# An attention head's 64-column copies ahead of the scores, its key turned in the scores' run, and two more tiles parked in DRAM

## The chip, the cores and the metric

The kernel runs on one core of a Trainium2 chip. Its time is the device time of one execution in microseconds. TensorE (PE, with its weight loads as PEld) does the matmuls, VectorE (DVE) and ScalarE (ACT) the elementwise work, GpSimd (POOL) and SyncE (SP) mostly issue DMA transfers. Each engine runs its own instruction stream in program order and waits for the others by semaphores.

## The reference

One layer of a decoder trunk, T = 1024 positions, D = 1024 channels, float32:

```
h = rms_norm(x, norm_w) * (1 + scale) + shift        # shift, scale, gate from c
hq, hf, hi, hz, gq, gk, gv, gz, ga, mg = split(h @ w_in)
HGRN, 8 heads, key 128, value 128:  f = lb + (1 - lb) * sigmoid(hf);  k = (1 - lb) * sigmoid(-hf);  q = silu(hq);  v = hi
GLA,  4 heads, key 128, value 256:  alpha = sigmoid(ga @ alpha_w + alpha_b) ** (1/16);  q = gq / sqrt(128);  k = gk;  v = gv
both: S_t = diag(decay_t) S_(t-1) + k_t v_t^T,   o_t = S_t^T q_t          # decay is f or alpha
y = rms_norm(o) * silu(z);   u = y @ w_branch
merged = sigmoid(mg_h) * u_h + sigmoid(mg_g) * u_g
out = rms_norm(x + gate * (merged @ w_out), final_norm_w)
```

The reference walks the recurrence in chunks of 64 positions. The kernel works with chunks of 128 (NCH = 8 of them) and splits them further, as told below.

## The kernel before

**Big matmuls.** A float32 product is taken as three fp32r products of high and low parts. The high part is a cast on ACT (L211), the low part a subtraction on DVE (L212). The input projection runs as a list of jobs (`Stream.jobs`); each job loads its weights with SP, splits them, and does runs of matmuls of 128 x 512 (L607, L2000), six of them to a unit. The branch products (L1422) and the output product (L1599) follow. All feature-major tiles of 128 x 1024 float32 live in 46 slots of SBUF (`Slots`, `S.get` and `S.free`); loads and splits of the next jobs (`Stream.ahead`) are only started while enough slots are free.

**Side work.** Between the units, `Stream.weave` advances generators. A generator gives back by `yield n` for how many units (divided by a pace of 1.08, for HGRN heads 1.15) it wants to be left alone. The twelve attention heads, four of GLA and then eight of HGRN, are such generators and run one after the other. A tile scheduler then sets the final order of the instructions on each engine; dependences become semaphore waits.

**One head** (`attention`, L639). q, k and the decays f stand feature-major, 128 x 1024. The scores within a chunk are built in levels, each with decays multiplied into q and k:

- L657 to L661: copies of q and products with decays go to the buffer `xb`; L665 is a run of matmuls for blocks of 4 positions.
- L667 to L694: q and k grow by decays, evictions into `blk`, the next products in `xb`; L698 is the run for blocks of 16.
- `keep(n)` copies the halves of k and q that face each other at level n with two ACT copies of 512 columns (L718) into `xb`. `grow(n)` then multiplies decays into k (L726), into q (L727), and shortens the totals (L729). In order: keep(16), grow(16), keep(32), grow(32).
- After waiting, and after `early` has asked for the values: three short runs of matmuls, for 16s (L756) and 32s (L762) on the copies, and for 64s (L767) on k and q themselves. Then grow(64), which has to wait for L767. Evictions: L771 on DVE, L776 (four) and L779 (two) on ACT, into `scT`.
- After `yield 3`: seven transposes of k (L791, TensorE against the identity) into two PSUM tiles, copied to `kT` by ACT (L792), and L795 (ACT). After `yield 2.5`: the state updates, L815 (kT times v) with L819 and L821 on DVE, and the outputs L834 and L836. For GLA, `inverse_root` follows (L992, L993 on TensorE, L994 and L995 on ACT, each behind a load of a table of functions).

**Other side work that shares the engines.** `alpha_side` makes the decays of the third and fourth GLA head: two DVE operations (L949, L950) per head, then on ACT exp (L953), ln (L956), exp (L960), both heads at each step. `gate_side` adds up the gate row with DVE operations (L1101, L1104), splits it (L202 on ACT, L203 on DVE) and sums it with four matmuls (L1112, L1113). `weight_sums` (L1266 to L1272, DVE) makes sums of weights for later. `gla_k_done` gets the key of a GLA head out of PSUM; of the fourth head (h = 3) it is written to DRAM and read back by `load_qk`, the third's stays in its slot. Decays of both stay in their slots (`alphas`).

Of the kernel before, what the change touches and what calls it, by code (L numbers as in the profile page):

```python
# [10 lines left out]
F32 = mybir.dt.float32  # L11
# [5 lines left out]
P = 128  # L17
D = 1024
T = 1024
KT = D // P  # L20
NCH = T // P
# [68 lines left out]
def hybrid_trunk_kernel(  # L90
# [6 lines left out]
    nc = tc.nc  # L97
# [541 lines left out]
    def attention(q, k, f, v, V, post, early, lead=3, next_up=None):  # L639
# [68 lines left out]
            return ap.rearrange("p (b two n) -> p b two n", two=2, n=n)  # L708

        flat = xb.rearrange("p b c -> p (b c)")  # L710
        kept = {}
        off = [320, tot[:, 256:320]]

        def keep(n):
            at = 0 if n == 16 else 1024
            kept[n] = flat[:, at:at + 512], flat[:, at + 512:at + 1024]
            for dst, src in zip(kept[n], (pairs(k, n)[:, :, 0, :], pairs(q, n)[:, :, 1, :])):
                nc.scalar.copy(dst.rearrange("p (b n) -> p b n", n=n), src)  # L718

        def grow(n):  # L720
            nb = T // (2 * n)
            at, cur = off
            cv = cur.rearrange("p (b two) -> p b two", two=2)
            left, right = cv[:, :, 0:1], cv[:, :, 1:2]
            qv, kv = pairs(q, n), pairs(k, n)
            TT(kv[:, :, 0, :], kv[:, :, 0, :], bc(right, [nb, n]), M)  # L726
            TT(qv[:, :, 1, :], qv[:, :, 1, :], bc(left, [nb, n]), M)  # L727
            nxt = tot[:, at:at + nb]
            TT(nxt.unsqueeze(2), left, right, M)  # L729
            off[:] = at + nb, nxt  # L730
# [13 lines left out]
        grow(16)  # L744
        keep(32)
        grow(32)
        yield 4
        early()
        yield 6 - lead
# [1 line left out]

        k16, q16 = kept[16]
        k32, q32 = kept[32]
        for b in range(32):
            ch, j = b // 4, b % 4
            nc.tensor.matmul(sc_ps[1][32 * j:32 * j + 16, ch * 16:ch * 16 + 16],  # L756
                             k16[:, b * 16:b * 16 + 16], q16[:, b * 16:b * 16 + 16], start=True, stop=True)
# [4 lines left out]
                nc.tensor.matmul(sc_ps[0][p0:p0 + 32, c0:c0 + 32], k32[:, i * 32:i * 32 + 32],  # L762
                                 q32[:, i * 32:i * 32 + 32], start=True, stop=True)
        for ch in range(NCH):
            s0 = ch * P
            p0, c0 = ch % 2 * 64, 128 + ch // 2 * 64
            nc.tensor.matmul(sc_ps[1][p0:p0 + 64, c0:c0 + 64], k[:, s0:s0 + 64],  # L767
                             q[:, s0 + 64:s0 + 128], start=True, stop=True)
        grow(64)
        cur = off[1]  # L770
        cpr(blk[:, :, 16:32], bc(masks[16], [NCH, 16]),  # L771
            sc_ps[1][:, 0:128].rearrange("p (c t) -> p c t", c=NCH))
        for hf in range(2):
# [5 lines left out]
            nc.scalar.copy(scT[0:64, odd::2, 64:128],  # L779
                           sc_ps[1][64 * odd:64 * odd + 64, 128:384].rearrange("p (c t) -> p c t", t=64))  # L780
        scoring.discard(me)
        yield 3


        kT = S.get([NCH, P])
        for g in range(2):
            nt = 4 if g == 0 else 3
            pt = mtile()
            for i in range(nt):
                ch = g * 4 + i  # L790
                nc.tensor.transpose(pt[:, i * P:(i + 1) * P], k[:, ch * P:(ch + 1) * P], ident)  # L791
            nc.scalar.copy(kT[:, g * 4:g * 4 + nt, :].rearrange("p c s -> p (c s)"), pt[:, 0:nt * P])  # L792
        S.free(k)
        for j in range(4):
            nc.scalar.copy(scT[32 * j:32 * j + 32, :, 32 * j:32 * j + 32], blk[32 * j:32 * j + 32])  # L795
        if next_up:
            next_up()
        yield 2.5
        per = 512 // V
        spp = 1024 // V  # L800
        st = [S.get([1024]) for _ in range((7 + spp - 1) // spp)]
# [107 lines left out]
    def alpha_half(half):  # L909
# [21 lines left out]
            nc.scalar.activation(alphas[h][:, sl], m[:, h, :], AF.Exp, scale=1.0 / TAU)  # L931
        S.free(z, m)

    def alpha_side(pair):
        zs = {}
        while len(S.free_list) < 6:
            yield 1
        for h in pair:
            zb = zs[h] = S.get([T])
            for th in range(2):  # L940
                pz = mtile()
                mm_alpha(pz, h, slice(th * 512, th * 512 + 512))
                nc.scalar.activation(zb[:, th * 512:(th + 1) * 512], pz, AF.Identity,
                                     bias=vec[:, R_AB + h:R_AB + h + 1])
            yield 2
        S.free(ga4, aw4)
        for h in pair:
            m = alphas[h] = S.get([T])
            nc.vector.tensor_scalar_min(m, zs[h], 0.0)  # L949
            nc.vector.scalar_tensor_tensor(zs[h], m, 2.0, zs[h], ALU.mult, ALU.subtract)  # L950
            yield 2
        for h in pair:
            nc.scalar.activation(zs[h], zs[h], AF.Exp)  # L953
        yield 3
        for h in pair:
            nc.scalar.activation(zs[h], zs[h], AF.Ln, bias=one_t)  # L956
            nc.vector.tensor_sub(alphas[h], alphas[h], zs[h])
            yield 2
        for h in pair:
            nc.scalar.activation(alphas[h], alphas[h], AF.Exp, scale=1.0 / TAU)  # L960
            S.free(zs[h])
        yield 3

    def silu_done(store, key):
# [80 lines left out]
                settle(qk, ("z", h, vh))  # L1045
        S.free(*sq.values())

    k3_d = dp.tile([P, T], F32, name="k3")

    def load_qk(h):  # L1050
        for f, key in ((h, "q"), (4 + h, "k")):
            if f < NG or h == 3:
                t = g_state[key, h] = S.get([T])
                nc.sync.dma_start(t, qk_d[f] if f < NG else k3_d)

    def gla_k_done(h):
        def f(ps):
            t = S.get([T])
            for th in range(2):
                nc.vector.tensor_copy(t[:, th * 512:th * 512 + 512], ps[th])  # L1060
            if h == 3:
                nc.gpsimd.dma_start(k3_d, t)
                S.free(t, sent=True)
            else:
                g_state[("k", h)] = t
        return f

    def col(c0, w=P):
# [1036 lines left out]
```

## Time and profile before

| | |
|---|---|
| runs | 1173.1, 1173.27, 1175.14 us (median 1173.27) |
| profiled execution | 1172.94 us, span 1171.2 us, granted clock 0.998 |
| busy | PE 98%, PEld 80%, DVE 72%, ACT 55%, POOL 12% of the span |
| seven transposes of a head (L791) | 84 in all, 11.1 us busy, 272 ns each |
| runs of L767 | 192 matmuls, 8.2 us busy, 228 ns each |
| ACT copies L718 | 0.62 us for 512 columns |
| DVE products L726, L727 | 0.69 us for 512 columns (mean) |

A row of the timeline has the start in us, the length, the engine, line and operation, the tile written and those read, and how many instructions the row joins; in brackets the time that the engine stood idle before it and what ended that. A row of the waits has who waited for what, the total in us, how often, and the longest.

### The profile page before, as it was taken

What the parts mean: (1) busy time and instruction counts of PE and PEld (TensorE: products, weight loads), DVE (VectorE), ACT (ScalarE), POOL (GpSimd) and SP (SyncE); (2) the same over time, 40 slices, a digit from 0 to 9 for tenths busy, and PEclk for the clock granted to TensorE, in tenths of its full rate; (3) what the DMA queues carried; (4) which work ended last, traced back from release to release, by engine and by line L of the source; (5) the groups of instructions that cost most, each with busy time, mean ns of one, the idle gap of its engine ahead of it and who ended that gap; (6) DMA issues with size and microseconds to landing.
All of it is one profiled execution on the core that took longest, in us unless ns stands there. A gap on an engine that the chain in (4) does not pass through costs nothing.

```text
span 1171.2 us, 20559 instructions
## 1 busy us (share of the span) xinstructions
PE 1147.1 (98%) x8089; PEld 942.8 (80%) x8089; DVE 841.5 (72%) x1316; ACT 646.4 (55%) x963; POOL 138.2 (12%) x285
## 2 busy tenths in 40 slices
PE   7999999999999999999999999999999999999997
PEld 5777888888778888788888888888888888888886
DVE  4755677676696636887697797595643866988994
ACT  5675464374574758646455446566643644534654
POOL 5121111010111101222211110001110000000000
PEclk9999999999999999999999999999999999999999
DMA  9847359486676546988766955146799746435523
GB/s 319 285 150 246 147 187 314 146 270 234 216 239 210 173 153 204 294 280 272 261 211 196 304 168 166 57 167 215 236 313 302 264 162 214 128 108 163 186 91 136
DMA packets 155986, 245.56 MB, mean 210 GB/s; under 512 B 10139, under 2 KB 107473, under 8 KB 155890
## 3 DMA queue, kind: packets, MB, share of 16 engines
q1 hardware_dynamic: 134866, 174.10, 47.3%
q0 software_dynamic: 20976, 70.15, 15.7%
q8 instruction: 63, 1.03, 0.4%
q14 instruction: 33, 0.27, 0.1%
q10 hardware_dynamic: 48, 0.01, 0.0%
HBM read 170.29 MB, written 73.92 MB: 209 GB/s over the span
## 4 chain that ended last, share of the span: by engine, by line
PE 81%; DVE 7%; ACT 7%; DMA 2%; issue 2%; SPq 1%; ACTq 0%; DVEq 0%
PE pd L607 18%; PE pd L2000 15%; PE pd L1422 14%; PE sc_ps L1422 6%; PE pm L1422 6%; PE pd L396 3%; PE pd L1599 3%; PE pm L834 2%; PE pm L836 2%; PE sc_ps L1599 2%; PE sc_ps L815 2%; PE sc_ps L396 1%; PE pm L1599 1%; ACT b L211 1%; DMA b<-in_ada_w_dram 1%
## 5 line engine op out<-in xcount | busy, mean ns | idle before, releaser
L607 PE MATMUL pd<-b,b 128*128 128x512 f32 x1248 | 299.7, 395 | 0.0
L607 PEld LDWEIGHTS pd<-b,b 128*128 128x128 f32 x1248 | 230.4, 188 | 48.8
L2000 PE MATMUL pd<-b,b 128*128 128x512 f32 x1008 | 238.5, 394 | 3.9 <-ACT b L211 2.4
L2000 PEld LDWEIGHTS pd<-b,b 128*128 128x128 f32 x1008 | 187.4, 188 | 46.0 <-ACT b L211 2.8
L1422 PE MATMUL pd<-b,b 128*128 128x512 f32 x720 | 169.4, 390 | 0.0
L1422 PEld LDWEIGHTS pd<-b,b 128*128 128x128 f32 x720 | 134.8, 188 | 28.2
L212 DVE TENSOR_TENSOR b<-b,b 128x1024 fp32r<-128x1024 f32 x92 | 110.7, 1220 | 55.0 <-ACT b L211 53.5
L1365 DVE TENSOR_TENSOR b<-b,b 128x1024 fp32r<-128x1024 f32 x56 | 68.1, 1220 | 55.1 <-ACT b L1364 43.7
L211 ACT CAST b<-b 128x1024 fp32r<-128x1024 f32 x92 | 93.6, 1047 | 18.0 <-DMA v<-b 4.1
L1364 ACT CAST b<-b 128x1024 fp32r<-128x1024 f32 x56 | 58.5, 1050 | 67.8 <-PE pm L1422 17.0
L1422 PE MATMUL sc_ps<-b,b 128*128 128x512 f32 x324 | 77.5, 390 | 0.1
L1342 DVE TENSOR_TENSOR b<-b,b 128x1024 fp32r<-128x1024 f32 x48 | 57.9, 1219 | 25.8 <-ACT b L1341 21.1
L1341 ACT CAST b<-b 128x1024 fp32r<-128x1024 f32 x48 | 49.9, 1049 | 42.8 <-PE pd L1422 15.8
L1422 PE MATMUL pm<-b,b 128*128 128x512 f32 x300 | 71.1, 389 | 0.0
L1422 PEld LDWEIGHTS sc_ps<-b,b 128*128 128x128 f32 x324 | 60.6, 188 | 12.9 <-ACT scT L779 0.5
L1422 PEld LDWEIGHTS pm<-b,b 128*128 128x128 f32 x300 | 56.3, 188 | 11.7
L203 DVE TENSOR_TENSOR b<-b,b 128x1024 fp32r<-128x1024 f32 (+1 forms) x37 | 35.7, 976 | 27.5 <-ACT b L202 27.3
L396 PE MATMUL pd<-b,b 128*128 128x512 f32 x192 | 51.8, 402 | 0.9 <-ACT b L202 0.8
L1274 POOL DMA_DIRECT2D ws<-b x64 | 34.6, 540 | 132.6 <-DVE b L1266 48.8
L726 DVE TENSOR_TENSOR b<-b,tot 128x512 f32<-128x512 f32 x36 | 24.7, 686 | 31.2 <-PE sc_ps L767 29.7
L834 PE MATMUL pm<-scT,b 128*128 128x128 f32 x256 | 46.8, 275 | 0.0
L396 PEld LDWEIGHTS pd<-b,b 128*128 128x128 f32 x192 | 34.3, 188 | 11.9 <-ACT b L202 1.8
(337 smaller groups left out, 1752.9 us busy)
## 6 DMA issues: line engine op xcount, KB each, us to landing
b<-in_w_in_dram SPq DMA_DIRECT2D x64, 512.0 KB, 6.1
ws<-b POOLq DMA_DIRECT2D x64, 256.0 KB, 5.1
b<-ws SPq DMA_DIRECT2D x32, 512.0 KB, 4.0
b<-in_w_in_dram SPq DMA_DIRECT2D x52, 256.0 KB, 4.5
b<-fx SPq DMA_DIRECT2D x24, 512.0 KB, 4.5
b<-in_x_dram SPq DMA_DIRECT2D x16, 512.0 KB, 6.1
b<-in_ada_w_dram SPq DMA_DIRECT2D x32, 256.0 KB, 6.4
v<-b POOLq DMA_DIRECT2D x32, 256.0 KB, 3.6
```

What stands on the lines that cost most here:

```text
L211: held(nc.scalar.copy(hi, src))
L212: nc.vector.tensor_sub(lo, src, hi.bitcast(F32))
L396: nc.tensor.matmul(accs[f], wg(a, d, f), b[d][:, half * 512:half * 512 + 512], start=(d == 0 and n == 0), stop=(d == KT - 1 and n == 2))
L607: nc.tensor.matmul(ps[th][0:w, :], a[:, k, 0:w], b[:, th * 512:(th + 1) * 512], start=(k == 0 and n == 0), stop=(k == KT - 1 and n == 2))
L834: nc.tensor.matmul(o, vch(ch)[:, vh * P:(vh + 1) * P], scT[:, ch, :], start=True, stop=(ch == 0))
L1341: nc.scalar.copy(hi, src)
L1342: nc.vector.tensor_sub(lo, src, hi.bitcast(F32))
L1364: nc.scalar.copy(hi, t)
L1365: nc.vector.tensor_sub(lo, t, hi.bitcast(F32))
L1422: nc.tensor.matmul(o, a[:, sl], c, start=(p in (1, 5) and kt == 0 and n == 0), stop=(kt == 3 and n == 2), skip_group_check=True)
L1599: nc.tensor.matmul(o, a, b, start=(p in (1, 5) and kt == 0 and n == 0), stop=(kt == 3 and n == 2), skip_group_check=True)
L2000: nc.tensor.matmul(st.bank[i], l_[:, i * P:(i + 1) * P], r_, start=(p in (1, 5) and kk == 0 and a == 0 and n == 0), stop=(kk == 1 and a == ...
```

## The change

It has three parts. `keep(64)` copies the 64-column halves into a buffer of its own (`wide`, one slot), and grow(64) follows at once, both directly behind grow(32); the matmuls of the 64s read the copies. The seven transposes come directly behind the matmuls of the 64s, in the same run on TensorE, so they read k after grow(64); their copies to kT come behind the score copies, and the two waits of 3 and 2.5 become one of 4. The third GLA head's key goes through DRAM as the fourth's did, and the fourth head's decay goes there too; `load_qk` reads them back.

```diff
--- before.py
+++ after.py
@@ -708,12 +708,16 @@
             return ap.rearrange("p (b two n) -> p b two n", two=2, n=n)
 
         flat = xb.rearrange("p b c -> p (b c)")
-        kept = {}
+        kept, wide = {}, []
         off = [320, tot[:, 256:320]]
 
         def keep(n):
-            at = 0 if n == 16 else 1024
-            kept[n] = flat[:, at:at + 512], flat[:, at + 512:at + 1024]
+            if n == 64:
+                wide.append(S.get([2, 512]))
+                kept[n] = wide[0][:, 0], wide[0][:, 1]
+            else:
+                at = 0 if n == 16 else 1024
+                kept[n] = flat[:, at:at + 512], flat[:, at + 512:at + 1024]
             for dst, src in zip(kept[n], (pairs(k, n)[:, :, 0, :], pairs(q, n)[:, :, 1, :])):
                 nc.scalar.copy(dst.rearrange("p (b n) -> p b n", n=n), src)
 
@@ -744,6 +748,9 @@
         grow(16)
         keep(32)
         grow(32)
+        keep(64)
+        grow(64)
+        cur = off[1]
         yield 4
         early()
         yield 6 - lead
@@ -751,6 +758,7 @@
 
         k16, q16 = kept[16]
         k32, q32 = kept[32]
+        k64, q64 = kept[64]
         for b in range(32):
             ch, j = b // 4, b % 4
             nc.tensor.matmul(sc_ps[1][32 * j:32 * j + 16, ch * 16:ch * 16 + 16],
@@ -762,12 +770,19 @@
                 nc.tensor.matmul(sc_ps[0][p0:p0 + 32, c0:c0 + 32], k32[:, i * 32:i * 32 + 32],
                                  q32[:, i * 32:i * 32 + 32], start=True, stop=True)
         for ch in range(NCH):
-            s0 = ch * P
             p0, c0 = ch % 2 * 64, 128 + ch // 2 * 64
-            nc.tensor.matmul(sc_ps[1][p0:p0 + 64, c0:c0 + 64], k[:, s0:s0 + 64],
-                             q[:, s0 + 64:s0 + 128], start=True, stop=True)
-        grow(64)
-        cur = off[1]
+            nc.tensor.matmul(sc_ps[1][p0:p0 + 64, c0:c0 + 64], k64[:, ch * 64:ch * 64 + 64],
+                             q64[:, ch * 64:ch * 64 + 64], start=True, stop=True)
+        S.free(*wide)
+        kT = S.get([NCH, P])
+        turned_k = []
+        for g in range(2):
+            pt = mtile()
+            for i in range(4 - g):
+                ch = g * 4 + i
+                nc.tensor.transpose(pt[:, i * P:(i + 1) * P], k[:, ch * P:(ch + 1) * P], ident)
+            turned_k.append(pt[:, 0:(4 - g) * P])
+        S.free(k)
         cpr(blk[:, :, 16:32], bc(masks[16], [NCH, 16]),
             sc_ps[1][:, 0:128].rearrange("p (c t) -> p c t", c=NCH))
         for hf in range(2):
@@ -779,23 +794,13 @@
             nc.scalar.copy(scT[0:64, odd::2, 64:128],
                            sc_ps[1][64 * odd:64 * odd + 64, 128:384].rearrange("p (c t) -> p c t", t=64))
         scoring.discard(me)
-        yield 3
-
-
-        kT = S.get([NCH, P])
-        for g in range(2):
-            nt = 4 if g == 0 else 3
-            pt = mtile()
-            for i in range(nt):
-                ch = g * 4 + i
-                nc.tensor.transpose(pt[:, i * P:(i + 1) * P], k[:, ch * P:(ch + 1) * P], ident)
-            nc.scalar.copy(kT[:, g * 4:g * 4 + nt, :].rearrange("p c s -> p (c s)"), pt[:, 0:nt * P])
-        S.free(k)
+        for g, pt in enumerate(turned_k):
+            nc.scalar.copy(kT[:, g * 4:g * 4 + 4 - g, :].rearrange("p c s -> p (c s)"), pt)
         for j in range(4):
             nc.scalar.copy(scT[32 * j:32 * j + 32, :, 32 * j:32 * j + 32], blk[32 * j:32 * j + 32])
         if next_up:
             next_up()
-        yield 2.5
+        yield 4
         per = 512 // V
         spp = 1024 // V
         st = [S.get([1024]) for _ in range((7 + spp - 1) // spp)]
@@ -931,6 +936,8 @@
             nc.scalar.activation(alphas[h][:, sl], m[:, h, :], AF.Exp, scale=1.0 / TAU)
         S.free(z, m)
 
+    alpha3_d = dp.tile([P, T], F32, name="alpha3")
+
     def alpha_side(pair):
         zs = {}
         while len(S.free_list) < 6:
@@ -959,6 +966,9 @@
         for h in pair:
             nc.scalar.activation(alphas[h], alphas[h], AF.Exp, scale=1.0 / TAU)
             S.free(zs[h])
+        if 3 in pair:
+            nc.gpsimd.dma_start(alpha3_d, alphas[3])
+            S.free(alphas.pop(3), sent=True)
         yield 3
 
     def silu_done(store, key):
@@ -1045,24 +1055,23 @@
                 settle(qk, ("z", h, vh))
         S.free(*sq.values())
 
-    k3_d = dp.tile([P, T], F32, name="k3")
+    k_d = {h: dp.tile([P, T], F32, name=f"k{h}") for h in (2, 3)}
 
     def load_qk(h):
         for f, key in ((h, "q"), (4 + h, "k")):
-            if f < NG or h == 3:
-                t = g_state[key, h] = S.get([T])
-                nc.sync.dma_start(t, qk_d[f] if f < NG else k3_d)
+            t = g_state[key, h] = S.get([T])
+            nc.sync.dma_start(t, qk_d[f] if f < NG else k_d[h])
+        if h == 3:
+            alphas[h] = S.get([T])
+            nc.sync.dma_start(alphas[h], alpha3_d)
 
     def gla_k_done(h):
         def f(ps):
             t = S.get([T])
             for th in range(2):
                 nc.vector.tensor_copy(t[:, th * 512:th * 512 + 512], ps[th])
-            if h == 3:
-                nc.gpsimd.dma_start(k3_d, t)
-                S.free(t, sent=True)
-            else:
-                g_state[("k", h)] = t
+            nc.gpsimd.dma_start(k_d[h], t)
+            S.free(t, sent=True)
         return f
 
     def col(c0, w=P):
```

In the changed file the lines shift: keep's copy is L722, grow's products L730, L731 and L733, the three score runs L764, L770 and L774, the transposes L783, the score copies L791 and L794, the kT copies L798, L815 becomes L820; exp, ln, exp of `alpha_side` are L960, L963 and L967; the gate's sums L1110, L1113, L1121 and L1122; L1147 becomes L1156, L969 becomes L979, L657 to L698 keep their numbers.

How this moves instructions: first an HGRN head on ACT, the seventh head of twelve, from keep(16) to the copies of kT. Before:

```order
L718 COPY xb<-b_5134 128x512
L718 COPY xb<-b_5252 128x512
L776 COPY scT<-sc_ps_72 32x4x32 x4
L657 COPY xb<-b_5599 128x32x32
L1147 ACT_TABLE_LOAD
L1147 ACTIVATE b_5713<-b_5601 128x1024
L779 COPY scT<-sc_ps_73 64x4x64 x2
L969 ACT_TABLE_LOAD
L969 ACTIVATE b_5570<-pd_0_5434 128x512
L969 ACTIVATE b_5570<-pd_1_5435 128x512
L792 COPY b_5583<-pm_5584 128x512
L792 COPY b_5583<-pm_5590 128x384
```

With the change:

```order
L722 COPY xb<-b_5229 128x512
L722 COPY b_5409<-b_5111 128x512
L211 CAST b_5421<-b_5169 128x1024
L722 COPY b_5409<-b_5229 128x512
L979 ACTIVATE b_5460<-pd_0_5332 128x512
L979 ACTIVATE b_5460<-pd_1_5333 128x512
L1156 ACT_TABLE_LOAD
L1156 ACTIVATE b_5681<-b_5568 128x1024
L791 COPY scT<-sc_ps_72 32x4x32 x4
L794 COPY scT<-sc_ps_73 64x4x64 x2
L798 COPY b_5543<-pm_5544 128x512
L798 COPY b_5543<-pm_5549 128x384
```

The two copies to `b_5409` (the `wide` buffer) are new and stand ahead of the scores; the sigmoid of the next head with its table load and the activations L979 moved ahead of the score copies, and the kT copies follow these directly. On TensorE, counted in big matmuls: from the scores to the transposes there were 12 and from these to L815 12 to 15 (18 in the fifth head); now the transposes stand behind the scores and 18 matmuls lie between them and L815, in a GLA head 24. From one HGRN head to the next it was 144 matmuls and is now 132 in most.

Second, ACT in the third head's stretch, where `alpha_side` runs beside the head. Before:

```order
L953 ACT_TABLE_LOAD
L953 ACTIVATE b_2242<-b_2242 128x1024
L691 COPY xb<-b_2155 128x64x4
L692 COPY xb<-b_2155 128x64x2x4
L211 CAST b_2377<-b_2174 128x1024
L953 ACTIVATE b_2272<-b_2272 128x1024
L956 ACT_TABLE_LOAD
L956 ACTIVATE b_2242<-b_2242,ones 128x1024
L956 ACTIVATE b_2272<-b_2272,ones 128x1024
L211 CAST b_2503<-b_2284 128x1024
L960 ACT_TABLE_LOAD
L960 ACTIVATE b_2362<-b_2362 128x1024
```

With the change:

```order
L960 ACT_TABLE_LOAD
L960 ACTIVATE b_2251<-b_2251 128x1024
L691 COPY xb<-b_2148 128x64x4
L692 COPY xb<-b_2148 128x64x2x4
L211 CAST b_2382<-b_2190 128x1024
L963 ACT_TABLE_LOAD
L963 ACTIVATE b_2251<-b_2251,ones 128x1024
L960 ACT_TABLE_LOAD
L960 ACTIVATE b_2277<-b_2277 128x1024
L963 ACT_TABLE_LOAD
L963 ACTIVATE b_2277<-b_2277,ones 128x1024
L211 CAST b_2515<-b_2289 128x1024
```

Where both heads' exponentials stood together and both logarithms after them, they now alternate. With the load for L967, which comes next, that makes five table loads where there were three. The six copies L722 of the head follow behind them.

Third, TensorE in the tenth head, where the sums of `gate_side` stand. Before, behind L698:

```order
L698 MATMUL sc_ps_72<-xb,b_6506 32x48 x32
L607 MATMUL pd_0_6833<-b_140,b_6690 128x512
L607 MATMUL pd_1_6834<-b_140,b_6690 128x512
L1112 MATMUL pm_6842<-b_6750,ones_r 128x512
L1113 MATMUL pm_6842<-b_6751,ones_r 128x512
L1112 MATMUL pm_6846<-b_6750,ones_r 128x512
L1113 MATMUL pm_6846<-b_6751,ones_r 128x512
```

With the change, in the run of the scores, 30 big matmuls behind L698:

```order
L764 MATMUL sc_ps_73<-xb 16x16 x32
L770 MATMUL sc_ps_72<-xb 32x32 x16
L1121 MATMUL pm_6888<-b_6845,ones_r 128x512
L1121 MATMUL pm_6892<-b_6845,ones_r 128x512
L774 MATMUL sc_ps_73<-b_6822 64x64 x5
L1122 MATMUL pm_6888<-b_6846,ones_r 128x512
L1122 MATMUL pm_6892<-b_6846,ones_r 128x512
L774 MATMUL sc_ps_73<-b_6822 64x64 x2
```

Between L698 and the scores lay 42 matmuls of 128 x 512, four of them the gate's; now 30 lie there, and the gate's four stand among the 64s. On DVE the gate's sums (L1110, L1113) moved along, from ahead of L698 to behind it, ahead of the products of grow(32) and grow(64).

## The prediction

> **What bounds the kernel now.** The page comes first: span, busy shares, and by engine the chain of work that ended last.
>
> ```profile
> span 1171.2 us, 20559 instructions
> PE 1147.1 (98%) x8089; PEld 942.8 (80%) x8089; DVE 841.5 (72%) x1316; ACT 646.4 (55%) x963; POOL 138.2 (12%) x285
> PE 81%; DVE 7%; ACT 7%; DMA 2%; issue 2%; SPq 1%; ACTq 0%; DVEq 0%
> ```
>
> TensorE is busy for 98% of the span and 81% of the chain is its own. The change adds and removes no matmul, so it can only move the moments at which TensorE stands still. Second view: what TensorE (PE) and its weight loads (PEld, from 105 us on) waited for: total, times, longest.
>
> ```profile
> PE pd L2000 <- ACT b L211: 2.4, 1, 2.4
> PE sc_ps L665 <- DVE xb L661: 2.3, 2, 1.4
> PE sc_ps L815 <- ACT b L792: 2.1, 6, 0.5
> PE sc_ps L698 <- DVE xb L694: 1.2, 2, 0.8
> ...
> PEld sc_ps L815 <- ACT b L792: 4.2, 7, 0.9
> PEld sc_ps L665 <- ACT b L211: 3.1, 2, 1.8
> PEld pd L2000 <- ACT b L211: 2.8, 1, 2.8
> PEld sc_ps L1422 <- ACT scT L779: 0.5, 1, 0.5
> PEld sc_ps L767 <- DVE b L726: 0.3, 1, 0.3
> ```
>
> The PE rows understate a stall, because the modelled end of the matmul before reaches into it; the PEld rows overstate it by what the load ahead would have hidden. Together these rows say that some 11 us of standing is within reach of the attention heads, and that is all there is to win. Third view: the timeline of an ordinary HGRN head (the seventh), TensorE, then ACT, then DVE.
>
> ```profile
> 566.19 0.89 PE L698 MATMUL sc_ps<-xb,b 128*32 128x48 f32 x64
> 567.01 9.81 PE L607 MATMUL pd<-b,b 128*128 128x512 f32 x42
> 577.72 0.69 PE L767 MATMUL sc_ps<-b,b 128*64 128x64 f32 x16
> 581.89 3.69 PE L607 MATMUL pd<-b,b 128*128 128x512 f32 x15
> 586.06 1.83 PE L815 MATMUL sc_ps<-b,b 128*128 128x128 f32 x14 [0.48 <-ACT b L792]
> ...
> 571.06 0.62 ACT L718 COPY xb<-b 128x512 f32<-128x512 f32 x1 [0.33 <-DVE b L726]
> 577.85 1.06 ACT L776 COPY scT<-sc_ps 32x128 f32<-32x128 f32 x4 [6.17 <-PE sc_ps L762]
> 582.38 0.75 ACT L779 COPY scT<-sc_ps 64x256 f32<-64x256 f32 x2
> 585.42 0.97 ACT L792 COPY b<-pm 128x512 f32<-128x512 f32 x2
> ...
> 571.75 0.68 DVE L726 TENSOR_TENSOR b<-b,tot 128x512 f32<-128x512 f32 x1
> ```
>
> One big matmul costs 9.81 / 42 = 0.23 us, my ruler below. grow(32) ends at 571.75 + 0.68 = 572.43; L767 starts at 577.72, 5.29 us later. The copies of the turned keys start at 585.42 and end just as L815 may start.
>
> **The change part by part.**
>
> *Keys turned behind the scores.* L791 keeps its seven transposes, so nothing is saved on TensorE by moving them; only the distance to L815 counts. It was 12 to 15 matmuls and becomes 18 in an HGRN head and 24 in a gated one. The fifth head already has 18 in the kernel before (transposes end, then L815):
>
> ```profile
> 496.08 4.37 PE L607 MATMUL pd<-b,b 128*128 128x512 f32 x18
> 500.29 1.72 PE L815 MATMUL sc_ps<-b,b 128*128 128x128 f32 x14
> ```
>
> and L815 waits for nothing there. I let the L815 waits go in all heads: between the 2.1 and the 4.2 us of the two rows, and nearer to the second, since in head seven 15 matmuls from 581.89 are over at 585.3 and L815 starts at 586.06: **+3.9**. Should the new place of the kT copies, behind six score copies on ACT, make them late again, this is 0.
>
> *Copies of the 64s ahead of the scores.* Per head two copies of 0.62 us on ACT (L718's row) come to stand in front of the scores, and two products of 0.68 us on DVE move there. L767 then hangs on grow(32), then one copy (0.62): 572.43 + 0.62 = 573.1 against 577.72. It fits with 4.6 us to spare, and in the gated heads (36 matmuls between L698 and the scores, 8.3 us, instead of 42) with about 3. In steady heads I price it at 0. What hides it is that run of matmuls; without it, 0.62 for the copy and 0.68 for each late product per head. L767's own 0.3 goes: **+0.3**. The L1422 wait for L779 (0.5 in the row; the score copies now come earlier against the last stages) goes too: **+0.3**. DVE's long idle time ahead of the old grow(64) cost nothing, as DVE is not on TensorE's path there.
>
> *Third head's key and fourth's decay through DRAM.* The nearest rows are the fourth head's key:
>
> ```profile
> k<-b POOLq DMA_DIRECT2D x1, 512.0 KB, 5.7
> b<-k SPq DMA_DIRECT2D x1, 512.0 KB, 5.1
> ```
>
> Two more such stores on POOL's queue and two loads on SP's. Each load is issued a whole head (over 100 matmuls, 23 us) ahead of its reader, against 5.1 us to land. Behind them on SP's queue stand the value loads and sum factors, which have that much lead as well: 0. If a load were late, the head's first product would wait, up to 5 us, once.
>
> *What the shorter heads do to the order.* This is where most of the sum lies: the side work runs earlier, and at four places the waits change.
>
> Fourth head (L665, L2000):
>
> ```profile
> 308.07 0.85 PE L665 MATMUL sc_ps<-xb,b 128*32 128x80 f32 x34 [1.39 <-DVE xb L661]
> 323.71 0.49 PE L2000 MATMUL pd<-b,b 128*128 128x512 f32 x1 [2.38 <-ACT b L211]
> ...
> 317.30 1.28 ACT L994 ACT_TABLE_LOAD   x1
> 322.61 1.05 ACT L211 CAST b<-b 128x1024 fp32r<-128x1024 f32 x1
> ```
>
> The cast for the next weights was queued on ACT behind L994 and L995, two table loads and three evaluations, from 317.30 to 323.66, and L2000 waited. In the new order the inverse root comes 38 matmuls earlier and the head's query is asked for 100 matmuls ahead of L665 instead of 25, so both stalls go: between 1.39 + 2.38 = 3.8 and 1.8 + 2.8 = 4.6, **+4.0**. But the casts of another job now stand behind the same ACT work: 323.66 − 317.30 = 6.4, one more cast and its DVE half about 1.2 each, 8.8 in all against 32 to 36 matmuls (7.4 to 8.3). What is late next is that L2000: between 0 and 2.4, I take the upper middle, **−1.4**.
>
> Third head (scores, with the fourth head's decay woven in):
>
> ```profile
> 251.26 1.28 ACT L953 ACT_TABLE_LOAD   x1 [2.52 <-DVE b L950]
> 252.56 1.06 ACT L953 ACTIVATE b<-b 128x1024 f32<-128x1024 f32 x1
> 256.37 1.28 ACT L956 ACT_TABLE_LOAD   x1
> 265.95 0.62 ACT L718 COPY xb<-b 128x512 f32<-128x512 f32 x1 [0.29 <-DVE b L726]
> 267.51 0.70 PE L756 MATMUL sc_ps<-xb 128*16 128x16 f32 x64
> ```
>
> The last copy ends at 266.57, 0.94 before the scores. The change parts the two exponentials, so exp, ln, exp, ln stand on ACT instead of exp, exp, ln, ln: two more table loads, 2.56 us, ahead of the copies; about 1 us of it falls into time that ACT idled. So the 16s are ready 1.5 later, at 266.6 instead of 265.1 (the middle of the four copies). From there the chain runs product, copy, product, copy, copy, product: 32s at 266.6 + 0.62 + 0.68 = 267.9, 64s at 267.9 + 0.68 + 1.24 and some hand-over = 270.2, the turned key at 271. TensorE stands six matmuls (1.4 us) earlier in the order and comes at 266.0; then, each time after what it waited for, at 267.3, 268.3 and 270.9. The stalls are 0.6, 0.6, 1.9 and 0.1: **−3.2**, bounds 0 (ACT's idle time takes it all) and 4.4.
>
> [...]
>
> Tenth head:
>
> ```profile
> 698.02 0.89 PE L698 MATMUL sc_ps<-xb,b 128*32 128x48 f32 x64 [0.79 <-DVE xb L694]
> 690.72 1.20 DVE L1104 TENSOR_TENSOR b<-b,b 1x1024 f32<-1x1024 f32 x1
> 686.97 1.31 DVE L1101 SCALAR_TENSOR_TENSOR b<-b,cs,b 128x1024 f32<-128x1024 f32 x1
> 696.86 0.68 DVE L1266 TENSOR_TENSOR b<-b 128x512 f32<-128x512 f32 x1
> 691.96 1.05 ACT L202 CAST b<-b 128x1024 fp32r<-128x1024 f32 x1 [0.66 <-DVE b L1104]
> ```
>
> The gate's sums (L1101, L1104) stood ahead of L698 on DVE, and L698 waited 0.79. They are now behind L698: **+0.8**. There they stand ahead of grow(16), grow(32) and the 64s: two L1101 (2.6), three weight sums of 0.68 (2.0), L1104 (1.2) and L202 on ACT ahead of the copies (1.05), 6.9 us. Head seven's own chain took 572.43 − 566.19 = 6.2 with some 1.8 of such foreign work in it, so 4.4 + 0.62 + 6.9 = 11.9 from L698 to the 64s. TensorE is there after 0.89 + 30 × 0.23 + the 16s and 32s (about 1) + two ones matmuls 0.46 = 9.3. Stall 2.6, and a little for the second product of the ones: **−2.8**, bounds 0 and 4.
>
> Fifth head: 15 matmuls instead of 21 lie between L698 and the 16s, with one weight sum less on DVE. 4.4 + 2 × 0.68 + 0.62 = 6.4 to the 64s, TensorE there after 0.89 + 23 × 0.23 + 1 = 7.2; but the 16s and 32s, due after 4.3 and 5.6, hang on the same chain and come about 0.4 late each: **−0.8**, bounds 0 and 1.5.
>
> **The sum:** 3.9 + 0.3 + 0.3 + 4.0 + 0.8 = 9.3 won; 1.4 + 3.2 + 2.8 + 0.8 = 8.2 lost; 1.1 faster. The profiled execution took 1172.94 (span 1171.2), the median shown is 1173.27, 0.3 above. 1172.94 − 1.1 = 1171.8; with small stalls inside runs that neither wait view names (entries that close up when the heads get shorter), I say **1171.5**.
>
> **The rivals.**
>
> *A: the new stalls don't come.* DVE and ACT are 28% and 45% idle and may run ahead of where I put them. Then 9.3 is won and 1.4 at most lost: 1172.94 − 9.3 = 1163.6 to 1165. Half of it gives 1168. For it: in the kernel before, the chains of heads seven and five end well ahead of the scores. Against it: in heads three and ten the order on the engine itself puts the foreign work ahead.
>
> *B: slower, the late 64s.* In every head L767 now hangs on the end of the chain L698, grow(16), grow(32), copy. It decides where the foreign work on DVE and ACT inside that chain passes the spare 4.6 us (HGRN) or 3 us (gated). The order puts 3 to 4 us of it into heads six to eight, against 1.8 before, so 2 to 3 us are left there. If it decides in the twelve heads at 0.7 each (a late product), that is 8.4 more lost: 1171.8 + 8.4 = 1180; in half of them 1176.
>
> [...]
>
> *D: the turned keys are still late.* The kT copies stand on ACT behind the six score copies (1.06 + 0.75 us in head seven's rows), and weight casts may come between. If L815 waits as before, 3.9 isn't won: 1175.7.
>
> **How the numbers follow.** What a measurement here can tell from no change is about 0.2%, 2.35 us: 1170.9 to 1175.6. My forecast has 0.36, with its own range 1169 to 1174: of it 0.12 lies below 1170.9, 0.22 within, 0.02 above. A 0.26, all faster. B 0.20, all slower. C 0.06, within. D 0.10, half within, half slower. The 0.02 left goes to faster. Faster 0.12 + 0.26 + 0.02 = 0.40; within 0.22 + 0.06 + 0.05 = 0.33; slower 0.02 + 0.20 + 0.05 = 0.27. The range, 1166 to 1177.5, takes in most of A and the lower half of B.
>
> **What would show it.** Right: no row of L815 waiting for the kT copies; no L665 wait in head four; L774 (the new 64s) waiting for ACT copies in heads three and ten only, some 2 us each; five table loads in the third head's stretch. A: no such rows for L774. B: L774 or L783 among the PE waits with eight or more times. [...] D: L820 (the new L815) waiting for L798. What would make the forecast wrong is above all a stall in a place that I read from the order as covered: a weight cast on ACT behind the copies that moved ahead.

## The result and the profile after

The changed kernel is slower: 1179.03 us (median of 12 executions, 1176.04 to 1181.2) against 1175.22 for the kernel before, measured beside it (12 executions, 1173.1 to 1176.66). The ratio is 1.0035, 95% interval 1.0026 to 1.0043. The forecast was 1171.5, faster or the same, with a range up to 1177.5.

The page of the changed kernel, its first two lines, and then what TensorE waited for (total, times, longest; where dots stand, rows of the first 30 us and rows on which nothing here rests are left out):

```profile
span 1178.4 us, 20599 instructions
PE 1149.5 (98%) x8089; PEld 946.2 (80%) x8089; DVE 843.1 (72%) x1315; ACT 662.4 (56%) x990; POOL 140.6 (12%) x287
...
PE sc_ps L665 <- DVE xb L661: 2.4, 2, 1.6
...
PE pd L2009 <- ACT b L1867: 2.3, 1, 2.3
PE sc_ps L774 <- ACT b L722: 1.6, 2, 1.3
PE sc_ps L770 <- DVE blk L746: 1.1, 1, 1.1
...
PE pm L1121 <- ACT b L202: 1.1, 1, 1.1
PE sc_ps L698 <- DVE xb L694: 0.9, 2, 0.6
...
PE sc_ps L770 <- ACT xb L722: 0.6, 1, 0.6
PE sc_ps L764 <- ACT xb L722: 0.4, 1, 0.4
```

The wait of L815 (now L820) for the turned keys is gone, and the waits of the third and tenth heads stand where the prediction put them. But the waits do not make the 7.2 us between the two profiled spans: from 30 to 1100 us TensorE stands for 12.7 us, against 10.0 before, and the first 50 us take 0.5 longer. What is left shows in the column PEclk of the busy times in chosen stretches (start and end, length, then busy time with the number of instructions for PE, PEld, DVE, ACT and POOL, then the granted TensorE clock, DMA share and GB/s). The three stretches hold the third head's scores, the fourth head's inverse root, and the tenth head's scores. Before:

```profile
265.00:280.00 15.00, 14.55 (x172) 11.74 (x171) 14.34 (x23) 7.53 (x17) 2.67 (x5) 1.00 0.84 297
317.00:327.00 10.00, 7.62 (x59) 5.75 (x59) 5.82 (x13) 9.94 (x14) 2.47 (x5) 1.00 0.57 205
700.00:715.00 15.00, 15.00 (x176) 12.33 (x175) 9.51 (x20) 8.66 (x15) 1.62 (x3) 1.00 0.67 196
```

After:

```profile
265.00:280.00 15.00, 12.24 (x150) 9.96 (x150) 12.83 (x22) 9.64 (x21) 3.19 (x6) 0.77 0.90 298
317.00:327.00 10.00, 7.68 (x27) 5.75 (x25) 7.32 (x12) 4.56 (x6) 3.23 (x6) 0.83 0.86 292
700.00:715.00 15.00, 13.03 (x155) 9.48 (x155) 11.31 (x22) 12.73 (x25) 2.16 (x4) 0.89 0.54 148
800.00:1100.00 300.00, 300.00 (x1347) 249.15 (x1346) 209.77 (x225) 150.94 (x191) 16.62 (x31) 1.00 0.64 213
```

The clock fell from 1.00 to 0.77, 0.83 and 0.89 in these three places and is 1.00 in the last stages. 0.23 of 15 us, 0.17 of 10 us and 0.11 of 15 us are 3.5, 1.7 and 1.7 us of clock, 6.9 in all, some 0.6 of it while TensorE stood anyway. (With 2.7 us of standing that is more than the spans differ. The PE rows understated the L815 waits that went, 2.1 against 4.2 in the PEld rows, which may account for the rest.) The timeline of TensorE at the third head's scores shows how it comes about:

```profile
266.95 0.70 PE L764 MATMUL sc_ps<-xb 128*16 128x16 f32 x64 [0.37 <-ACT xb L722]
268.73 0.46 PE L770 MATMUL sc_ps<-xb 128*32 128x32 f32 x32 [1.09 <-DVE blk L746]
270.49 1.12 PE L774 MATMUL sc_ps<-b 128*64 128x64 f32 x16 [1.30 <-ACT b L722]
271.54 1.76 PE L783 MATMUL pm<-ident,b 128*128 128x128 f32 x7
272.95 7.26 PE L607 MATMUL pd<-b,b 128*128 128x512 f32 x24
```

Three stalls, 2.8 us together within 4 us. The granted clock fell when the first two were over and the third had just begun:

```profile
268.00:269.30 1.30, 0.46 (x32) 0.38 (x32) 1.30 (x4) 0.41 (x2) 0.00 (x0) 1.00 1.04 425
269.40:270.40 1.00, 0.00 (x0) 0.00 (x0) 1.00 (x4) 1.00 (x3) 0.00 (x0) 0.50 1.01 406
```

From L774 on, everything takes nearly twice as long: L774 1.12 where L767 took 0.69, the transposes 1.76 where they took 0.93, and the 24 big matmuls 7.26 where they take 5.73 at full clock (experiment 1); in the single records their starts lie 0.427 us apart until 276.1, and 0.227 from there. The fourth head's stall was ended by an eviction (L1867), which stands on ACT behind L1004, L1005 and two weight casts and waited another 0.47 us for a low part on DVE (L212). It is followed by the same: 20 matmuls in 6.42 us, where 20 at 0.227 take 4.5.

```profile
319.97 6.42 PE L2009 MATMUL pd<-b,b 128*128 128x512 f32 x20 [2.32 <-ACT b L1867]
```

### The profile page after: what moved, and what is told of

It reads as the page before. It is cut to its first block, busy times and chain, and to the rows that moved or that the text cites. A ratio compares the mean times of both kernels' runs of the same rounds, so it can differ in the third digit from the quotient of the medians.

```text
span 1178.4 us, 20599 instructions
## 1 busy us (share of the span) xinstructions
PE 1149.5 (98%) x8089; PEld 946.2 (80%) x8089; DVE 843.1 (72%) x1315; ACT 662.4 (56%) x990; POOL 140.6 (12%) x287
## 4 chain that ended last, share of the span: by engine, by line
PE 72%; issue 15%; DVE 4%; ACT 3%; DMA 3%; POOL 1%; SPq 1%; POOLq 0%; ACTq 0%; DVEq 0%
PE pd L607 19%; PE pd L1431 14%; PE pd L2009 7%; PE sc_ps L1431 6%; PE pm L1431 6%; PE pd L396 3%; PE pd L1608 3%; PE sc_ps L1608 2%; PE pm L839 1%; PE sc_ps L396 1%; PE pm L1608 1%; PE pm L841 1%; PE sc_ps L820 1%; DMA b<-in_ada_w_dram 1%; DMA b<-in_w_in_dram 1%
## 5 line engine op out<-in xcount | busy, mean ns | idle before, releaser
L212 DVE TENSOR_TENSOR b<-b,b 128x1024 fp32r<-128x1024 f32 x92 | 110.7, 1221 | 71.9 <-ACT b L211 71.7
L1351 DVE TENSOR_TENSOR b<-b,b 128x1024 fp32r<-128x1024 f32 x48 | 57.8, 1220 | 19.7 <-ACT b L1350 15.2
L722 ACT COPY xb<-b 128x512 f32<-128x512 f32 x48 | 29.6, 619 | 50.9 <-DVE b L700 19.9
```

The lines of the kernel that those rows point to most:

```text
L212: nc.vector.tensor_sub(lo, src, hi.bitcast(F32))
L1351: nc.vector.tensor_sub(lo, src, hi.bitcast(F32))
```

## The experiments

The theory, called "order": the shorter wait behind the scores moves foreign work into the third, fourth and tenth heads, and the stalls there, with the clock that falls behind them, cost more than the removed waits. Rivals: the copies of the 64s ahead of the scores cost in every head ("copies"), or the two tiles in DRAM do ("DRAM").

**1. The third head's table loads.** In `alpha_side`:

```diff
         for h in pair:
-            nc.scalar.activation(zs[h], zs[h], AF.Exp)
+            held(nc.scalar.activation(zs[h], zs[h], AF.Exp))
         yield 3
         for h in pair:
-            nc.scalar.activation(zs[h], zs[h], AF.Ln, bias=one_t)
+            held(nc.scalar.activation(zs[h], zs[h], AF.Ln, bias=one_t))
```

> The changed kernel with alpha_side's two exponentials and two logarithms held in program order, so that they stand exp, exp, ln, ln again (three table loads instead of five) and behind most of the third head's copies. Theory 'order': the third head's stalls (0.4 + 1.1 + 1.3 us) and the half-clock stretch of some 4 us behind them go, together 6 to 7 us; against the kernel before 0.9975 (2.5 to 3 us faster). Rival 'copies': the time is lost to the copies or the DRAM tiles in every head; then it stays at 1.003.

Measured: 1.0003 (0.9993 to 1.0012), median 1176.08 against 1174.92. Three table loads, no stall at the scores, and no fall of the clock (TensorE, then the same stretch of busy times):

```profile
266.61 0.70 PE L764 MATMUL sc_ps<-xb 128*16 128x16 f32 x64
267.58 0.69 PE L774 MATMUL sc_ps<-b 128*64 128x64 f32 x16
268.93 5.73 PE L607 MATMUL pd<-b,b 128*128 128x512 f32 x24
276.68 1.13 PE L820 MATMUL sc_ps<-b,b 128*128 128x256 f32 x4 [1.15 <-ACT scT L794]
...
265.00:280.00 15.00, 13.85 (x170) 11.22 (x169) 10.53 (x13) 14.81 (x23) 3.36 (x7) 1.00 0.84 291
```

The gain is 0.0032 of the kernel before, 3.8 us, not 6 to 7: the exponentials and logarithms, held back, push the last exponentials (L967) with their table load ahead of a score copy (L794), and L820 waits 1.15 in the same head.

**2. The tenth head's gate sums.** The gate's generator starts earlier:

```diff
-        stream.more.append([gate_side(), 4, 1, 300])
+        stream.more.append([gate_side(), 4, 1, 270])
```

> The changed kernel with gate_side begun 30 units earlier, so that its sums stand in the eighth and ninth heads, ahead of the products that a run of the scores waits for. Theory 'order': the tenth head's stalls (0.6 + 1.05 + 0.3 + 0.7 us) and the short half-clock stretch behind them go, 3.5 to 4.5 us; against the kernel before 1.000. Rival 'copies': 1.003.

Measured: 0.9995 (0.9985 to 1.0005). 0.0040 below the change, 4.7 us, a little more than expected. The stretch from 700 to 715 us is back at full clock:

```profile
700.00:715.00 15.00, 14.93 (x181) 12.00 (x180) 8.41 (x16) 11.24 (x21) 2.16 (x4) 1.00 0.68 198
```

**3. Both edits.**

> Both edits together. Theory 'order': 10 to 11 us under the changed kernel, 0.994 of the kernel before, that is the 9 us which the old waits were worth less the fourth head's new one. Rival 'copies': 1.003.

Measured: 0.9972 (0.9961 to 0.9983), 7.4 us below the change (0.0063) and short of the 0.994. The two add up nearly (0.0032 + 0.0040 = 0.0072). The fourth head's stall and the clock behind it are left, which neither edit touches, and so are the L665 waits and a new wait of L820:

```profile
PE sc_ps L665 <- DVE xb L661: 2.4, 2, 1.6
PE pd L2009 <- ACT b L1867: 2.3, 1, 2.3
PE sc_ps L820 <- ACT scT L794: 1.0, 1, 1.0
...
317.00:327.00 10.00, 9.39 (x92) 7.44 (x93) 6.23 (x11) 4.67 (x8) 2.68 (x5) 0.83 0.89 312
```

**4. The old distance.** One number of the change put back to the sum of the old two waits:

```diff
             next_up()
-        yield 4
+        yield 5.5
         per = 512 // V
```

> The changed kernel with the wait behind the scores put back to 5.5 units, the sum of the old two, so that heads keep their old distance of 144 matmuls and the order of everything around them stays nearly that of the kernel before. Theory 'order': the L820 waits are gone (3.9 us), no new stall in the third and tenth heads, the fourth head's old stalls stay: 0.9965 (4 us faster). Rival 'copies': the copies ahead of the scores are still there: 1.003, with waits of L774 in many heads.

Measured: 0.9939 (0.9927 to 0.9951), median 1168.37, and executions within 0.4 us of each other. This version beats both kernels, by 6.5 us the one before. All of the change is in it but the shorter wait; so the shorter wait alone costs the change 0.0096, 11 us. Its waits (all over 0.5 us outside the start):

```profile
PE pm L1002 <- ACT b L202: 1.4, 1, 1.4
PE sc_ps L665 <- DVE xb L661: 0.9, 1, 0.9
PE pd L2009 <- DVE b L364: 0.8, 1, 0.8
PE sc_ps L698 <- ACT b L202: 0.6, 1, 0.6
```

Neither the L815 wait nor the fourth head's 2.4 is left, and from 30 to 1100 us the granted clock is 1.00. The rival "copies" falls: the 64s are copied ahead of the scores in all twelve heads here too, and L774 waits 0.4 us, once.

**5. The change without the DRAM tiles.** `attention` of the change in the kernel before, `alpha_side`, `load_qk` and `gla_k_done` as they were.

> The kernel before with the change to the heads alone (early copies of the 64s, turned keys behind the scores, waits of 3 + 2.5 made one of 4), without the two tiles in DRAM. Its order on ACT, DVE and TensorE is that of the whole change, with five table loads in the third head and the gate's sums in the tenth. Theory 'order': as slow as the whole change, 1.003. Rival 'DRAM': the stores and loads cost something: 1.000 or less here.

Measured: 1.0050 (1.0036 to 1.0064): as slow as the whole change or slower. Its profile has the same three stalls at the third head's scores (0.40, 1.09 and 1.30), but this time the clock did not fall there (1.00 from 265 to 280 us); it fell at the fourth and tenth heads (0.97 from 300 to 360 us, 0.94 from 680 to 740):

```profile
265.00:280.00 15.00, 12.22 (x163) 10.01 (x162) 14.46 (x26) 10.09 (x21) 2.27 (x5) 1.00 0.70 235
```

**6. The DRAM tiles alone.** The kernel before with only the parts of the diff in `alpha_side`, `load_qk` and `gla_k_done`.

> The kernel before with only the third head's key and the fourth's decay in DRAM. Theory 'order': 1.000, within 1 us. Rival 'DRAM': 1.003.

Measured: 0.9965 (0.9952 to 0.9977), median 1170.78, spread 0.44 us. Both theories were wrong here: the tiles in DRAM make the kernel 4 us faster. The waits tell where: the rows of L665 (2.3 us, 1.4 of them in the fourth head) and L2000 (2.4, now L2004) fall to

```profile
PE sc_ps L815 <- ACT b L792: 2.4, 6, 0.7
...
PE sc_ps L665 <- DVE xb L661: 0.9, 1, 0.9
...
PE pd L2004 <- ACT b L1862: 0.2, 1, 0.2
```

and one new wait comes, 1.2 us ahead of the inverse root's L997. (The profiled spans differ by 2.4 us; the 4 us of the medians hold, besides, the scatter of the kernel before, whose profiled execution was one of its fastest.) In the kernel before, half of the fourth head's L665 stands ahead of the third head's inverse root, where its products are late; with the tiles in DRAM the head begins a little later and L665 stands in one piece behind the inverse root.

**7. The shorter distance alone.** One number in the kernel before, behind the scores:

```diff
         scoring.discard(me)
-        yield 3
+        yield 1.5
```

> The kernel before with one number changed: the wait of 3 units behind the scores is 1.5, so that heads follow each other as closely as in the change; no early copies, no moved transposes, no DRAM tiles. Theory 'order': the shorter distance alone brings the five table loads into the third head and the gate's sums into the tenth, with the stalls and half-clock stretches, and the L815 waits stay: 1.004 to 1.007. Rival 'copies': without the copies ahead of the scores nothing is late: 1.000.

Measured: 1.0063 (1.0050 to 1.0075), as "order" expected. With no early copies, no moved transposes and no DRAM tiles, the third head has the alternating table loads and the late copies of the change (ACT, then TensorE):

```profile
254.37 1.28 ACT L956 ACT_TABLE_LOAD   x1
256.84 1.28 ACT L953 ACT_TABLE_LOAD   x1
259.21 1.28 ACT L956 ACT_TABLE_LOAD   x1
...
267.00 0.69 PE L756 MATMUL sc_ps<-xb 128*16 128x16 f32 x64 [0.39 <-ACT xb L718]
268.79 0.46 PE L762 MATMUL sc_ps<-xb 128*32 128x32 f32 x32 [1.09 <-DVE blk L742]
269.89 0.69 PE L767 MATMUL sc_ps<-b,b 128*64 128x64 f32 x16 [0.65 <-DVE b L727]
```

Two things came otherwise than expected. The L815 waits for the kT copies did not stay (0.2 in all). And the clock fell behind the third head alone (0.89 from 265 to 280 us, against 1.00 from 317 to 327 and from 700 to 715); most of this version's loss is standing, 15.2 us from 30 to 1100 us against 10.0 before, with 2.0 of it ahead of L756 in the fifth head.

**8. The copies without the moved transposes.** The kernel of experiment 4, but with the seven transposes and their copies at their old place, behind a wait of 3 and ahead of one of 2.5.

> The change without the moved transposes: the 64s are copied ahead of the scores and grow(64) follows at once, the DRAM tiles are there, but the transposes stand where they stood, behind a wait of 3, and a wait of 2.5 follows. Theory 'order': the copies are covered and the L815 waits (3.9 us) stay, so this shows what the moved transposes are worth beside the 0.9939 of the kernel with both and the old distance: 0.997. Rival 'copies': 1.003, L774 waits in many heads.

Measured: 0.9955 (0.9942 to 0.9967), median 1169.53. Against 0.9965 for the tiles alone, the early copies are worth 1 us or nothing (the intervals overlap), and against 0.9939 with the transposes moved, these are worth 0.0016, 1.9 us, or less (these intervals overlap too). Both together, experiment 6 against 4, are worth 0.0026, 3 us, with intervals that do not overlap. (The first and the second four ran on different chips, each beside its own runs of the kernel before.)

**9 to 11. A late copy that was no stall.** In the kernel of experiment 4, for the eighth head only, each copy of the 64s made m times more (m = 6, 7, 8):

```diff
                 nc.scalar.copy(dst.rearrange("p (b n) -> p b n", n=n), src)
+                if n == 64 and me == 8:
+                    for _ in range(6):
+                        nc.scalar.copy(dst.rearrange("p (b n) -> p b n", n=n), src)
```

> The fast kernel with the old distance (1168.4, spread 0.4 us), with the copy of each half of the 64s made six times more than needed in one HGRN head (the eighth of the twelve): 12 copies at about 0.51 us each behind one another, 6.1 us, against 4.9 us that the 64s had to spare before L774. One stall of about 1.2 us on TensorE. Theory 'clock' (a stall takes TensorE's granted clock down to half for some 3 us behind it, in the more of the executions the longer it is): at 1.2 us hardly, 1169.6. Rival 'stall only': a stall costs its own length, 1169.6.

> The same with seven more copies of each half: a stall of about 2.2 us. Theory 'clock': part of the executions lose up to 2 us more, times spread from 1170.6 to 1172.6. Rival 'stall only': 1170.6 with a spread of 0.4.

> The same with eight more copies of each half: a stall of about 3.3 us. Theory 'clock': most executions lose 1.5 to 2.5 us more, median about 1173.5, with a half-clock stretch behind the eighth head's scores in the profile. Rival 'stall only': 1171.7 with a spread of 0.4.

Measured: 0.9952 (0.9939 to 0.9964), 0.9939 (0.9927 to 0.9952), 0.9940 (0.9926 to 0.9954): 1170.26, 1168.58 and 1168.52, no loss that grows with m; the executions spread over 1.6, 2.4 and 1.1 us. The design failed: the scheduler counts the copies and puts other matmuls ahead of the 64s, here with m = 8 fourteen of them:

```profile
616.27 0.46 PE L773 MATMUL sc_ps<-xb 128*32 128x32 f32 x32
616.66 3.49 PE L607 MATMUL pd<-b,b 128*128 128x512 f32 x14
620.23 0.69 PE L777 MATMUL sc_ps<-b 128*64 128x64 f32 x16
```

So these say nothing on the clock. They do say that late copies of the 64s cost little by themselves where the scheduler foresees them and has other matmuls: with seven and eight more the ratio is that of experiment 4.

**12 to 15. A stall of known length.** The same place, but the order on TensorE from the eighth head's scores to its L820 is held as written, and m activations of one element, exp and sigmoid in turn (each behind a table load), stand on ACT ahead of that head's copies (m = 0, 4, 5, 6; the cut shows these alone, with m = 5):

```diff
+            late_one = n == 64 and me == 8
+            if late_one:
+                for i in range(5):
+                    held(nc.scalar.activation(tick[:, 0:1], tick[:, 1:2], AF.Sigmoid if i % 2 else AF.Exp))
```

> The control of the three runs beside it: the changed kernel with the old distance (wait of 5.5), in which the order on TensorE from the scores of the eighth head to its L820 is held as written. Nothing waits there. Both theories: as without the hold, 0.9939 of the kernel before, with a spread under 1 us.

> The control with four one-element activations, exp and sigmoid in turn, each behind a table load, on ACT ahead of that head's copies of the 64s: about 4 x 1.45 = 5.8 us against 4.9 to spare, one stall of about 0.9 us on TensorE that no other work can fill. Theory 'clock': hardly a loss of clock at this length, 0.9 us above the control. Rival 'stall only': 0.9 us above it.

> The same with five: a stall of about 2.4 us. Theory 'clock': between 2.4 and 4.5 us above the control, spread over 2 us from execution to execution, granted clock down where the time is long. Rival 'stall only': 2.4 above it, spread as in the control.

> The same with six: a stall of about 3.9 us. Theory 'clock': 5.5 to 6.5 us above the control in nearly every execution, with a half-clock stretch of 3 to 4 us behind the eighth head's scores. Rival 'stall only': 3.9 above it.

| activations | idle ahead of the 64s (profile) | median, spread | above the control | ratio to before |
|---|---|---|---|---|
| 0 | none | 1168.12, 0.6 | | 0.9943 (0.9922 to 0.9964) |
| 4 | 0.33 us | 1168.15, 1.1 | 0.0 | 0.9945 (0.9930 to 0.9960) |
| 5 | 1.85 us | 1170.59, 3.0 | 2.5 | 0.9961 (0.9947 to 0.9975) |
| 6 | 3.51 us | 1173.14, 2.1 | 5.0 | 0.9981 (0.9972 to 0.9991) |

The stalls came out some 0.5 us shorter than meant. With six activations the loss is 1.5 us more than the stall, and the half clock is in the records: the 64s take 1.12 us and the transposes 1.76, against 0.69 and 0.98 in the control (TensorE, then busy times of two stretches):

```profile
620.21 1.12 PE L788 MATMUL sc_ps<-b 128*64 128x64 f32 x16 [3.51 <-ACT b L732]
621.26 1.76 PE L799 MATMUL pm<-ident,b 128*128 128x128 f32 x7
...
618.00:624.00 6.00, 3.79 (x27) 3.50 (x28) 2.79 (x5) 5.88 (x13) 1.09 (x2) 0.72 0.06 21
624.00:630.00 6.00, 6.00 (x34) 5.16 (x34) 2.96 (x6) 5.45 (x10) 0.54 (x1) 1.00 0.77 242
```

"Stall only" falls at this length. With five the median lies 0.6 us above the stall, and the executions spread over 3 us where the control's spread over 0.6; but the profiled execution is the median one and its clock is 1.00 in every stretch from 595 to 640 us, around the stall, so no loss of clock is shown at this length. With four there is no loss that can be told. The order on TensorE is the same in all four, so the traces can be set side by side: from L704 (the run for blocks of 16) of the eighth head to its L837 (the old L820) they take 18.45, 18.82, 20.35 and 23.50 us. Beyond the stall that is 0.0, 0.1 and 1.5 us more than the control.

## Why the prediction was wrong

By its own steps:

- *Keys turned behind the scores, +3.9.* The mechanism was right: no wait of L820 for the kT copies is left. The size was probably too high: experiments 8 and 4 differ by 0.0016, 1.9 us, with overlapping intervals, and 6 and 4, which have the early copies between them too, by 3 us. That is nearer to the PE row (2.1); I went towards the PEld row (4.2), on one head.
- *Copies of the 64s, 0 in steady heads; +0.3 for L767.* Right. L774 waits in the third and tenth heads alone, and experiments 4 and 9 to 11 show the copies covered. Rival B, late 64s in every head, fell.
- *DRAM tiles, 0.* Wrong: alone they are worth 4 us in the median, 2.4 between the profiles (experiment 6). I priced the transfers and nothing else; that they also move the fourth head's start, and with it the stalls of 1.4 and 2.4, I had booked to the shorter heads.
- *Fourth head, +4.0 and −1.4.* The old stalls went, as they do with the tiles alone. The new one is 2.3, at the bound of 2.4, not 1.4; what is late last is an eviction (L1867), behind the same ACT work and two weight casts, and not a cast itself.
- *Third head, −3.2.* The profile has stalls of 0.37, 1.09 and 1.30, 2.8 together, at the same three runs. *Tenth head, −2.8 and +0.8:* 0.6 ahead of L770, 1.05 ahead of L1121 and 0.31 ahead of L774, 2.0 together; the old wait of L698 is 0.3 (from 0.8). A wait of 0.82 ahead of this head's L665 is new, and the sum has nothing for it. *Fifth head, −0.8:* its L764 to L774 don't wait; L665 waits 1.58 (0.92 before). Most places were read rightly from the order, and the stalls are near their prices.
- *What failed is the sum, which has no term for the clock.* It counts a stall as its own length. Behind the third, fourth and tenth heads' stalls stand 3.5, 1.7 and 1.7 us of clock, 6.3 of them while TensorE worked, and that is about the gap: the changed kernel's span of 1178.4 less 6.3 would be 1172.1, against 1171.2 before. The executions say the same. Among the 12 of the change, time and granted clock go together: 1176.04 at 0.995, 1181.2 at 0.990. A straight line through them (0.72 us per us of lost clock) meets full clock at 1171.6 us; a line through 25 executions of the kernel before (0.62) meets it at 1171.8. Both are estimates, and the lines reach beyond what was measured: the first 30 us take clock in the profiles of both kernels (0.94 before, 0.89 after) and of experiments 1 to 8 (0.94 or 0.89). By them the two kernels would be about level at full clock, so the forecast gain of 1 us isn't shown there either. That the rest of the sum comes out so near is in part luck: L815 and the fourth head were booked too high, the fifth head's L665 too low and the tenth head's L665 not at all, the third and tenth heads' scores a little too dear.
- *The base.* The profiled execution of the kernel before (1172.94, clock 0.998) was one of its fastest. Its other executions reach 1179.03, with clocks down to 0.992. Perhaps the 2.4 us stall of its own fourth head draws the clock down in some of them. That is argued, not shown: the versions of experiments 4, 6, 8 and 12, without that stall, lie within 0.7 us each, but those of 9 to 11 and 13, without it as well, spread over 1.1 to 2.4, the execution of 1179.03 had 0.995, and no profile of a longer one was taken. In any case the median, 1175.22, lies 2.3 us above the execution that I took as the base.
- *C, a switch of tables that costs more than its load, 0.06 of the chances.* No run shows such a term. In the kernel before, the load at 251.26 ends at 252.54 and the exponential starts at 252.56. In experiment 15 a load and an activation of one element follow each other every 1.52 us, 1.28 of it the load and 0.20 the activation.

```profile
612.95 1.28 ACT L730 ACT_TABLE_LOAD   x1
614.24 0.20 ACT L730 ACTIVATE tick<-tick 128x1 f32<-128x1 f32 x1
614.46 1.28 ACT L730 ACT_TABLE_LOAD   x1
```

What stays open: why the tiles in DRAM move L665 in the scheduler's order was not followed further, and the residue between 0.9972 (experiment 3) and 0.9939 (experiment 4), 3.9 us, is put down to the fourth head's stall (2.3 against 0.2), its clock (1.7), the L820 wait of 1.0 and the L665 waits (2.4 against 0.9) from their rows, without a run that removes them at the short distance. Which stalls take the clock down in which execution is open too.

## What to carry to other kernels

When TensorE is the bound, price a stall as its length plus the clock that may fall with it: here nothing beyond the length in the profiles at 0.3 and 1.85 us, 1.5 us more at 3.5. Several short stalls within 4 us can cost clock as a long one does (3.5 us of clock behind the changed kernel's third head) or leave it alone (at 1.00 behind the same stalls in experiment 5). A pace or a wait that only spaces the work is not neutral: change it apart from the rest, because it re-deals the order of everything that runs beside it. And look at the scatter: where executions spread over 5 us with the granted clock, as in the change, look for stalls, and in more than one profile, since the quickest can hide their cost.

## What the runs showed of the hardware

A stretch at half TensorE clock came with stalls that were each shorter than 2.4 us: one of 2.32 in the fourth head, three of 0.60, 1.05 and 0.31 in the tenth, and in the third head three of 0.37, 1.09 and 1.30, where the clock fell as the third began (1.00 from 268.00 to 269.30 us, 0.50 from 269.40). It came with the one of 3.51 too (experiment 15, 0.72 from 618 to 624 us). It need not come: the stall of 2.38 in the profile of the kernel before, those of 0.40, 1.09 and 1.30 in experiment 5 and that of 1.85 in experiment 14 left the clock at 1.00. So like stalls cost clock in one profile and none in another; what decides it is not shown. In the profile of the changed kernel the granted clock stood at 0.50 for 6.8 us in the third head (269.4 to 276.2 us), 3.4 in the fourth (320.6 to 324.0) and 3.4 in the tenth (706.3 to 709.7). For experiment 15 an estimate from its lost clock, at the same 0.50, is 0.28 x 6 / 0.5 = 3.4 us.
